# Splitting the attention weights by input tile, with the norm gain folded into the split

## The chip, the cores and the metric

The kernel runs on one core of one Trainium2 chip. The metric is the device time of one execution in microseconds. Engines are named as in the profile: PE is TensorE, with PEld its weight loads; DVE is VectorE, ACT is ScalarE, POOL is GpSimd, and SP issues most DMAs. Each engine runs its instructions in the order in which they were put into its queue.

## The reference

A two-layer decoder trunk over 512 tokens of width 1024. Layer 0 is a gated linear recurrence with a convolutional feed-forward network. Layer 1 is differential attention over shared keys and values, then another such network, then a final norm. What the change touches is layer 1's attention:

```python
def shared_kv(x, kv_norm, kv_w):
    kv = rmsnorm(x, kv_norm) @ kv_w            # keys (8 heads, 2 x 64) and values (8 heads, 128)
...
q = (h @ w_q).reshape(B, T, DA_HEADS, 2, DA_HEAD_DIM) * (DA_HEAD_DIM ** -0.5)
s = jnp.einsum('bqhcd,bkhcd->bhcqk', qb, k) + bias
p = jax.nn.softmax(s, axis=-1)
attn = p[:, :, 0] - lam * p[:, :, 1]
o = jnp.einsum('bhqk,bkhv->bqhv', attn, v)
o = rmsnorm(o, subln_g) * (1.0 - lambda_init)
x = x + o.reshape(B, T, DA_VDIM_TOTAL) @ w_o
```

Here `h` is the stream normed with another gain than that of the keys and values. Both norms are `x * rsqrt(mean(x^2)) * g`, with `g` one factor for each of the 1024 input features. So `g` can be moved from the stream to the rows of the weight that multiplies it.

## The kernel before, in words

**Products in two parts.** Every large product is made from operands split in two: `hi` is the operand rounded to the fast matmul format, `lo` is what the rounding left. Three matmuls, hi x hi, lo x hi and hi x lo (lines 104 to 106), stand for one. The weights come from memory as float32 and are split on the core: ACT casts the high part (`whi`), and DVE subtracts it from the float to get the low part (`wlo`).

**Weights in attention.** One load is a staged tile `wst` of 128 x 1024 (the input features of one of 8 input tiles on the partitions, the columns of all 8 side by side for keys and queries; for values 4 input tiles of 256 columns; for the output weight two output tiles of 4 x 128). `stage` (line 75) issues the DMA on SP. Where a norm gain belongs to the weight, POOL then multiplies the whole tile by it in place (line 86). `Load.high` (line 758) casts all 1024 columns on ACT at line 760, `Load.low` (line 762) subtracts them on DVE at line 763. There are 8 key, 8 query, 8 value and 8 output loads. There are three `wst` buffers and three pairs of `whi` and `wlo`: `high_next` (line 785) begins a split only when fewer than three loads are split or in use.

**The order of the work.** The attention stage is written in one fixed order for PE, DVE, ACT and POOL (line 1039). A block `b` is one head's 128 query tokens; there are 8 x 4 blocks, and block `b % 4 = i` looks at `(i + 1) * 128` keys. In the turn of block `b` the code issues: the scores of block `b + 2` (matmuls, and on DVE the biased minimum at line 968); two units of product work; `weigh(b + 1)`, whose result `at` (line 989, DVE) is the weighted difference of the two softmax parts; `turn(b)`, which transposes `at` on PE (line 996) and copies `aT` to SBUF on ACT (line 998); the exponentials of block `b + 2` on ACT (line 974); three units; `gather(b)`, the product of `aT` and the values on PE (line 1009) with a sum of squares on ACT (line 1012); one unit. After the fourth block of a head, `close` copies the head's output (line 1031) and puts the 13 steps of its norm into a queue `chain` (`ome` at line 1032, `rs` at lines 160 to 166, and so on).

A *unit* is one input tile's part of a key, query, value or output product, three matmuls of 512 columns or six of 256. A key or query product has 8 units, a pair of heads' values 16. `units` (line 941) issues each unit and after it some follow-up work: up to three steps of `chain`, and the casts of keys and queries from the queue `side`. After a key product DVE evacuates it (`kq`, line 833); each of its two halves is cast twice to `kh`, once by ACT into its own partitions (line 854) and once by POOL into the other 64 partitions (line 855); DVE then takes the low parts `kl` (line 861). Queries have two casts on ACT (line 841) and two low parts on DVE (line 844).

The splits stand at fixed places of a block's turn: `low_next` before `turn`, `high_next` after the exponentials, `low_next` after `gather`, and another `high_next` if fewer than two loads are ready. Loads are taken in the order of the list `order`: for each pair of heads two keys and two queries, then the pair's two halves of values; after all pairs the output weights. The first three loads are split ahead of the fixed order, beside the end of the feed-forward stage before it.

Of the kernel before, what the change touches and what calls it, by code (L numbers as in the profile page):

```python
# [19 lines left out]
P = 128  # L20
T = 512
# [15 lines left out]
class Trunk:  # L37
# [34 lines left out]
        self.split(self.x[n], hi, lo, g)  # L72
        return hi, lo

    def stage(self, src, width=1024, gain=None, k0=0, cols=P):

        st = self.wp.tile([P, 1024], F32, tag="wst", name="wst", bufs=3)
        dst = st[:, :width]
        if len(src.shape) == 3:
            dst = dst.rearrange("p (n k) -> p n k", n=src.shape[1])  # L80
        self.nc.sync.dma_start(dst, src)
        if gain is not None:
            n = width // cols
            w = st[:, :width].rearrange("p (k c) -> p k c", k=n)
            g = self.gains[:, gain, k0:k0 + n].unsqueeze(2).broadcast_to([P, n, cols])
            self.nc.gpsimd.tensor_tensor(w, w, g, ALU.mult)
        return st

    def weight_tiles(self):
# [628 lines left out]
    def attention(self, xkv, acc, on_tile):  # L718
        tc, nc, a = self.tc, self.nc, self.a
        v, s = nc.vector, nc.scalar  # L720
        mm = nc.tensor.matmul
        with ExitStack() as ctx:
# [28 lines left out]
            class Load:  # L751
# [1 line left out]
                    me.src, me.gain, me.k0, me.cols = src, gain, k0, cols  # L753

                def stage(me):
                    me.st = self.stage(me.src, 1024, me.gain, me.k0, me.cols)

                def high(me):
                    me.w = self.weight_tiles()
                    s.copy(me.w[0], me.st)  # L760

                def low(me):
                    v.tensor_tensor(me.w[1], me.st, me.w[0].bitcast(F32), ALU.subtract)  # L763

            half = KD // 2

            def out_load(m, k0):
                return Load(a["w_o"][2 * m:2 * m + 2, :, k0 * P:(k0 + half) * P].rearrange("n p k -> p n k"))
# [9 lines left out]
            staged, ready, lows, live, todo = deque(), deque(), deque(), [], deque(order)  # L778

            def stage_next(most=3):  # L780
                while todo and len(staged) < most:
                    staged.append(todo.popleft())
                    staged[-1].stage()

            def high_next():
                if staged and len(live) + len(ready) < 3:
                    ready.append(staged.popleft())
                    ready[-1].high()
                    lows.append(ready[-1].low)

            def low_next():
                while lows:
                    lows.popleft()()

            def split_next():
                high_next()
                low_next()

            def take(load):
                low_next()  # L800
                assert ready and ready[0] is load
                live.append(ready.popleft())
# [28 lines left out]
            def evac(ps, scale=1.0):  # L831
                t = ap.tile([P, T], F32, tag="kq", name="kq")
                v.scalar_tensor_tensor(t, ps, scale, rb, ALU.mult, ALU.mult)
                return t

            def queries(h, ps):

                q = evac(ps, -0.125)
                t = qs[h] = ap.tile([P, 2, T], F32R, tag="qs", name="qs")
                for c, (own, other) in enumerate(parts):  # L840
                    side.append(lambda c=c, own=own: s.copy(t[own, c], q[own]))
                for c, (own, other) in enumerate(parts):
                    side.append(lambda c=c, own=own, other=other:
                                v.tensor_tensor(t[other, c], q[own], t[own, c].bitcast(F32), ALU.subtract))  # L844

            def keys(h, ps):

                k = evac(ps)
                hi = ap.tile([P, 2, T], F32R, tag="kh", name="kh")
                lo = kls[h % 2]  # L850
                ks[h] = hi, lo

                def high(c, own, other):
                    s.copy(hi[own, c], k[own])
                    nc.gpsimd.tensor_copy(hi[other, c], k[own])

                for c, (own, other) in enumerate(parts):
                    side.append(lambda c=c, own=own, other=other: high(c, own, other))
                for c, (own, other) in enumerate(parts):
                    side.append(lambda c=c, own=own:  # L860
                                v.tensor_tensor(lo[own, c], k[own], hi[own, c].bitcast(F32), ALU.subtract))  # L861
# [33 lines left out]
            def add(n, ps):  # L895
                v.tensor_tensor(self.x[n], self.x[n], ps, ALU.add)
# [44 lines left out]
            def units(n, most=1):  # L941
                for _ in range(n):
                    k = next(work, None)
                    if k is None:
                        return
                    if k in (1, 2):
                        stage_next()
                    some(most)


            blocks, heads = {}, {}
# [87 lines left out]
            with tc.manual_schedule(engines=ORDERED):  # L1039
                first = [(self.bank("sc"), take(w[0])) for w in (K[0], Q[0])]  # L1040
                steps, got = self.norm_steps(acc, "n1", "sc")
                self.proj_first(first, xkv, KD - 1, steps)
                live.clear()
                rb, rc = got[1]
                keys(0, first[0][0])
                queries(0, first[1][0])
                some(8)
                units(2)
                split_next()
                units(2)  # L1050
                split_next()
                units(U0 - 4)
                for b in range(-2, 4 * NH):
                    h, i = divmod(b + 2, 4)
                    if h < NH:
                        if i == 0 and h % 2 == 1 and h < NH - 1:
                            bias(h + 1)
                        powers = scores(b + 2)
                    else:
                        powers = lambda: None  # L1060
                    units(U1, 0)
                    if 0 <= b + 1 < 4 * NH:
                        weigh(b + 1)
                    if b < 0:
                        powers()
                        split_next()
                        units(U2 + U3)
                        continue
                    low_next()
                    turn(b)  # L1070
                    powers()
                    high_next()
                    units(U2, 2)
                    gather(b)
# [178 lines left out]
```

## Time and profile before

| | us |
|---|---|
| median of 3 runs | 1269.04 |
| lowest, highest | 1267.32, 1269.81 |
| the profiled execution's own time | 1269.33 |
| its span, first to last instruction | 1267.5 |
| PE busy in the span | 1235.7 |
| DVE busy | 872.0 |
| ACT busy | 569.1 |
| POOL busy | 110.0 |

The profile is that of one execution. The attention stage lies between 640 and 893 us of the span. In the profile's rows a group is written as line, engine, operation, output tile <- input tiles, shapes, count, then busy us and mean ns of one, then the idle time ahead of it and what ended it. A row of the waits reads: who waited, `<-` for whom, us in total, times, longest. A row of the time line reads: start, duration, engine, line, operation, tiles, shapes, count, and in brackets the idle time before it. A row of stretches reads: start and end, length, and for each engine its busy time and instruction count, then the granted TensorE clock (1.00 is full), DMA share and GB/s.

### The profile page before, as it was taken

How to read it: one execution, taken by the hardware profiler on the slowest of the kernel's cores; microseconds unless marked ns; L12 is line 12 of the kernel's file. 1: busy time of each engine (PE TensorE's matmuls, PEld its weight loads, DVE VectorE, ACT ScalarE, POOL GpSimd, SP SyncE). 2: the span in 40 equal slices, each digit the busy share in tenths (PEclk: the TensorE clock that was granted, in tenths of full speed). 3: DMA queues.
4: the chain of work that ended last, by engine and by line, in shares of the span. 5: the costliest groups of instructions: out<-in, count | busy, mean ns of one | idle time of the engine just before them, and what ended most of it. 6: DMA issues, size and time to landing. Idle time of an engine off the chain costs nothing.

```text
span 1267.5 us, 18031 instructions
## 1 busy us (share of the span) xinstructions
PE 1235.7 (97%) x6994; PEld 1043.4 (82%) x6994; DVE 872.0 (69%) x1627; ACT 569.1 (45%) x986; POOL 110.0 (9%) x93
## 2 busy tenths in 40 slices
PE   8999999999999999999999889999999999999997
PEld 7888898788888888888888778798788888888886
DVE  7978879587777777523367988876687777773223
ACT  5454555444444444322245446564454444442221
POOL 3000000020000000000243332201100000000001
PEclk9999999999999999999999899999999999999998
DMA  6223222142333333333322212222233333333322
GB/s 211 84 82 123 85 84 68 38 130 87 97 99 100 100 97 90 100 92 92 96 100 67 72 55 58 77 74 83 84 100 100 89 96 98 100 92 92 96 87 67
DMA packets 37965, 115.36 MB, mean 91 GB/s; under 512 B 4040, under 2 KB 9464, under 8 KB 37880
## 3 DMA queue, kind: packets, MB, share of 16 engines
q1 hardware_dynamic: 36984, 113.30, 29.3%
q8 instruction: 55, 0.90, 0.3%
q10 hardware_dynamic: 896, 0.92, 0.2%
q14 instruction: 30, 0.25, 0.1%
HBM read 112.09 MB, written 3.68 MB: 91 GB/s over the span
## 4 chain that ended last, share of the span: by engine, by line
PE 57%; issue 30%; DVE 9%; ACT 2%; DMA 0%; SPq 0%; POOL 0%; POOLq 0%; ACTq 0%; DVEq 0%
PE mm L106 16%; PE mm L104 16%; PE mm L105 16%; DVE wlo L763 1%; PE po L1009 1%; DVE wlo L60 1%; DVE kl L861 1%; DVE sc L968 1%; PE tp L996 1%; ACT whi L760 1%; PE sc L104 1%; PE sc L105 1%; PE sc L106 1%; DVE sd L459 1%; DVE qs L844 1%
## 5 line engine op out<-in xcount | busy, mean ns | idle before, releaser
L104 PE MATMUL mm<-xh,whi 128*128 128x512 f32 x1008 | 398.7, 396 | 0.1
L105 PE MATMUL mm<-xl,whi 128*128 128x512 f32 x1008 | 394.9, 392 | 2.5 <-DVE xl L63 2.4
L106 PE MATMUL mm<-xh,wlo 128*128 128x512 f32 x1008 | 395.0, 392 | 2.3 <-DVE wlo L60 2.3
L60 DVE TENSOR_TENSOR wlo<-wst,whi 128x1024 fp32r<-128x1024 f32 (+2 forms) x182 | 216.0, 1191 | 152.5 <-ACT whi L59 150.2
L59 ACT CAST whi<-wst 128x1024 fp32r<-128x1024 f32 (+2 forms) x182 | 182.2, 1006 | 239.9 <-PE mm L105 188.1
L106 PEld LDWEIGHTS mm<-xh,wlo 128*128 128x128 f32 x1008 | 189.9, 188 | 43.5 <-DVE wlo L60 3.4
L105 PEld LDWEIGHTS mm<-xl,whi 128*128 128x128 f32 x1008 | 190.3, 189 | 41.6 <-DVE xl L63 4.5
L104 PEld LDWEIGHTS mm<-xh,whi 128*128 128x128 f32 x1008 | 190.3, 189 | 38.1 <-ACT whi L59 0.4
L104 PE MATMUL mm<-hh,whi 128*128 128x512 f32 (+1 forms) x374 | 141.0, 377 | 0.0
L105 PE MATMUL mm<-hl,whi 128*128 128x512 f32 (+1 forms) x374 | 140.8, 377 | 0.0
L106 PE MATMUL mm<-hh,wlo 128*128 128x512 f32 (+1 forms) x374 | 140.8, 376 | 0.0
L669 DVE TENSOR_TENSOR u<-mm,rbc_f 128x512 f32<-128x512 f32 x88 | 60.2, 688 | 73.4 <-PE mm L106 73.4
L149 POOL TENSOR_TENSOR acc<-acc,sq 128x512 f32<-128x512 f32 x18 | 26.7, 1485 | 651.4 <-ACT sq L148 651.2
L105 PEld LDWEIGHTS mm<-hl,whi 128*128 128x128 f32 x374 | 70.4, 188 | 13.0
L104 PEld LDWEIGHTS mm<-hh,whi 128*128 128x128 f32 x374 | 70.4, 188 | 12.9
L106 PEld LDWEIGHTS mm<-hh,wlo 128*128 128x128 f32 x374 | 70.4, 188 | 12.8
L671 ACT ACTIVATE c<-u,pack 128x512 f32<-128x512 f32 x88 | 71.7, 819 | 7.8 <-DVE u L669 4.0
L104 PE MATMUL mm<-whi,xh 128*128 128x256 f32 x256 | 74.0, 290 | 0.0
L59 ACT CAST hh<-c 128x512 fp32r<-128x512 f32 x44 | 27.3, 621 | 102.9 <-DVE c L680 102.9
L105 PE MATMUL mm<-wlo,xh 128*128 128x256 f32 x256 | 72.6, 284 | 0.6 <-DVE wlo L763 0.6
L106 PE MATMUL mm<-whi,xl 128*128 128x256 f32 x256 | 72.5, 284 | 0.0
L673 DVE SCALAR_TENSOR_TENSOR c<-u,pack,c 128x512 f32<-128x512 f32 x88 | 66.1, 751 | 2.8
(259 smaller groups left out, 1714.1 us busy)
## 6 DMA issues: line engine op xcount, KB each, us to landing
wst<-in_w_up_dram SPq DMA_DIRECT2D x88, 512.0 KB, 3.6
wst<-in_w_down_dram SPq DMA_DIRECT2D x32, 512.0 KB, 3.5
wst<-in_w_fqg_dram SPq DMA_DIRECT2D x22, 512.0 KB, 3.8
wst<-in_w_kq_dram SPq DMA_DIRECT2D x16, 512.0 KB, 3.6
wst<-in_w_down_dram SPq DMA_DIRECT2D x16, 384.0 KB, 3.1
wst<-in_w_i_dram SPq DMA_DIRECT2D x8, 512.0 KB, 3.8
wst<-in_w_ao_dram SPq DMA_DIRECT2D x8, 512.0 KB, 3.7
wst<-in_w_v_dram SPq DMA_DIRECT2D x8, 512.0 KB, 3.8
```

The lines of the kernel that those rows point to most:

```text
L59: i = nc.scalar.copy(hi, x)
L60: j = nc.vector.tensor_tensor(lo, x, hi.bitcast(F32), ALU.subtract)
L104: mm(out, s[0], m[0], start=start, stop=False)
L105: mm(out, s[0], m[1], start=False, stop=False)
L106: mm(out, s[1], m[0], start=False, stop=stop)
L149: add = lambda engine=nc.vector: engine.tensor_tensor(acc, acc, sq, ALU.add)
L459: v.copy_predicated(dst, m, src)
L669: v.tensor_tensor(u[:, 2:], ps, rb, ALU.mult)
L671: s.activation(c, u[:, 2:], AF.Identity, bias=self.cb[:, layer, n:n + 1], scale=w(2))
L673: v.scalar_tensor_tensor(c, u[:, 0:T], w(0), c, ALU.mult, ALU.add)
L760: s.copy(me.w[0], me.st)
L763: v.tensor_tensor(me.w[1], me.st, me.w[0].bitcast(F32), ALU.subtract)
```

## The change

POOL no longer multiplies the weights by the gain, and no longer casts keys. A load is split in pieces, one for each input tile (128 columns for keys and queries, 256 for values; output weights, which have no gain, in two pieces of 512). ACT makes a high piece as `Identity(gain * wst)`, DVE a low piece as `gain * wst - whi`. `begin` takes the buffers of a load; `pieces` issues a given number of steps, a step being the next high piece and, one high piece later, a low piece. Each unit is followed by one step, and each block's turn has two more after `gather`; what is left when a product needs its load is issued at once by `take`. The casts of keys into the other 64 partitions go to ACT.

```diff
-    def stage(self, src, width=1024, gain=None, k0=0, cols=P):
+    def stage(self, src, width=1024):
...
-        if gain is not None:
-            n = width // cols
-            w = st[:, :width].rearrange("p (k c) -> p k c", k=n)
-            g = self.gains[:, gain, k0:k0 + n].unsqueeze(2).broadcast_to([P, n, cols])
-            self.nc.gpsimd.tensor_tensor(w, w, g, ALU.mult)
...
+                def begin(me):
+                    me.w = self.weight_tiles()
+                    me.highs = deque(range(1024 // me.cols))
+                    me.lows = deque(me.highs)
+
+                def place(me, k):
+                    g = 1.0 if me.gain is None else self.gain(me.gain, me.k0 + k)
+                    return (slice(k * me.cols, (k + 1) * me.cols), g)
 
                 def high(me):
-                    me.w = self.weight_tiles()
-                    s.copy(me.w[0], me.st)
+                    c, g = me.place(me.highs.popleft())
+                    s.activation(me.w[0][:, c], me.st[:, c], AF.Identity, scale=g)
 
                 def low(me):
-                    v.tensor_tensor(me.w[1], me.st, me.w[0].bitcast(F32), ALU.subtract)
+                    c, g = me.place(me.lows.popleft())
+                    v.scalar_tensor_tensor(me.w[1][:, c], me.st[:, c], g, me.w[0][:, c].bitcast(F32),
+                                           ALU.mult, ALU.subtract)
...
-                return Load(a["w_o"][...].rearrange("n p k -> p n k"))
+                return Load(a["w_o"][...].rearrange("n p k -> p n k"), cols=T)
...
-            def high_next():
+            def begin_next():
                 if staged and len(live) + len(ready) < 3:
                     ready.append(staged.popleft())
-                    ready[-1].high()
-                    lows.append(ready[-1].low)
-            def low_next():
-                while lows:
-                    lows.popleft()()
+                    ready[-1].begin()
+            def pieces(load, most):
+                for _ in range(most):
+                    if load.highs:
+                        load.high()
+                        if len(load.lows) - len(load.highs) < 2:
+                            continue
+                    if load.lows:
+                        load.low()
+            def pieces_next(most=1):
+                begin_next()
+                load = next((n for n in ready if n.lows), None)
+                if load is not None:
+                    pieces(load, most)
             def split_next():
-                high_next()
-                low_next()
+                begin_next()
+                for load in ready:
+                    pieces(load, 1024)
             def take(load):
-                low_next()
                 assert ready and ready[0] is load
+                pieces(load, 1024)
                 live.append(ready.popleft())
...
                 def high(c, own, other):
                     s.copy(hi[own, c], k[own])
-                    nc.gpsimd.tensor_copy(hi[other, c], k[own])
+                    s.copy(hi[other, c], k[own])
...
                     some(most)
+                    pieces_next()
...
-                    low_next()
                     turn(b)
                     powers()
-                    high_next()
                     units(U2, 2)
                     gather(b)
-                    low_next()
                     if b % 4 == 1 and b > 1:
                         back()
-                    if len(ready) < 2:
-                        high_next()
+                    pieces_next(2)
```

More of the change, by code (lines that the diff above doesn't have):

```diff
@@ L755, in stage @@
                 def stage(me):
-                    me.st = self.stage(me.src, 1024, me.gain, me.k0, me.cols)
+                    me.st = self.stage(me.src)
+                def begin(me):
[5 more added lines that the diff above has]
+                    return (slice(k * me.cols, (k + 1) * me.cols), g)
                 def high(me):
-                    me.w = self.weight_tiles()
-                    s.copy(me.w[0], me.st)
+                    c, g = me.place(me.highs.popleft())
+                    s.activation(me.w[0][:, c], me.st[:, c], AF.Identity, scale=g)
                 def low(me):
-                    v.tensor_tensor(me.w[1], me.st, me.w[0].bitcast(F32), ALU.subtract)
+                    c, g = me.place(me.lows.popleft())
+                    v.scalar_tensor_tensor(me.w[1][:, c], me.st[:, c], g, me.w[0][:, c].bitcast(F32),
+                                           ALU.mult, ALU.subtract)
             half = KD // 2
             def out_load(m, k0):
-                return Load(a["w_o"][2 * m:2 * m + 2, :, k0 * P:(k0 + half) * P].rearrange("n p k -> p n k"))
+                return Load(a["w_o"][2 * m:2 * m + 2, :, k0 * P:(k0 + half) * P].rearrange("n p k -> p n k"), cols=T)
             K = [[Load(a["w_kq"][2 * h], 2)] for h in range(NH)]
@@ L777, in attention @@
             order += O[0] + O[1]
-            staged, ready, lows, live, todo = deque(), deque(), deque(), [], deque(order)
+            staged, ready, live, todo = deque(), deque(), [], deque(order)
             def stage_next(most=3):
```

## The prediction

> **What bounds the kernel now.** I read the page first, then the waits of TensorE in the attention stage, then the time line where the waits lie, and last the groups of DVE and ACT in one stretch between them.
>
> ```profile
> PE 1235.7 (97%) x6994; PEld 1043.4 (82%) x6994; DVE 872.0 (69%) x1627; ACT 569.1 (45%) x986; POOL 110.0 (9%) x93
> ```
>
> TensorE is the bound. The edited code runs in the attention stage alone (640 to 893 us), so the change can only give back what TensorE loses there. Its waits in that window:
>
> ```profile
> PE tp L996 <- DVE at L989: 9.5, 5, 3.0
> PE po L1009 <- ACT aT L998: 3.8, 3, 1.5
> PE mm L105 <- DVE wlo L763: 0.6, 1, 0.6
> ```
>
> Together 13.9 us. After some of these waits the clock is low for a while, as the first two stretches below show (columns: PE, PEld, DVE, ACT, POOL busy; granted clock; DMA). The third holds the key and query products of one pair of heads.
>
> ```profile
> 672.10:675.30 3.20, 3.12 (x9) 2.54 (x10) 1.98 (x10) 1.40 (x5) 0.00 (x0) 0.53 0.00 0
> 704.90:714.30 9.40, 8.56 (x31) 6.96 (x32) 8.83 (x27) 6.40 (x15) 0.00 (x0) 0.64 0.26 75
> 737.20:774.40 37.20, 32.93 (x182) 27.70 (x182) 32.40 (x78) 20.75 (x56) 13.22 (x8) 1.00 0.25 69
> ```
>
> The clock costs at most (1 - 0.53) x 3.2 = 1.5 us and (1 - 0.64) x 9.4 = 3.4 us, 4.9 in all. Part of it falls into waiting, so I take 3. The ceiling of a gain is 13.9 + 4.9 = 18.8 us, my central value for it 16.9.
>
> Why does `at` come late? The longest wait of TensorE (2.96 us, ended at 705.03) with GpSimd and DVE before it:
>
> ```profile
> 705.03 0.44 PE L996 MATMUL tp<-pack,at 128*128 128x128 f32 x2 [2.96 <-DVE at L989]
> ...
> 693.23 1.89 POOL L86 TENSOR_TENSOR wst<-wst,gains 128x1024 f32<-128x1024 f32 x1 [4.55 <-DVE wlo L763]
> 695.18 2.51 POOL L855 CAST kh<-kq 64x512 fp32r<-64x512 f32 x2
> 697.77 4.07 POOL L86 TENSOR_TENSOR wst<-wst,gains 128x1024 f32<-128x1024 f32 x2
> ...
> 691.90 1.22 DVE L763 TENSOR_TENSOR wlo<-wst,whi 128x1024 fp32r<-128x1024 f32 x1
> 693.48 2.73 DVE L763 TENSOR_TENSOR wlo<-wst,whi 128x1024 fp32r<-128x1024 f32 x1 [0.35 <-ACT whi L760]
> 696.12 2.11 DVE L861 TENSOR_TENSOR kl<-kq,kh 64x512 fp32r<-64x512 f32 x2
> 698.27 1.75 DVE L1032 TENSOR_SCALAR ome<-oms 128x4 f32<-128x4 f32 x1
> 700.05 1.82 DVE L160 TENSOR_SCALAR rs<-ome 128x4 int32<-128x4 int32 x1
> 704.49 0.48 DVE L989 SCALAR_TENSOR_TENSOR at<-p,r 128x256 f32<-128x256 f32 x1
> ```
>
> Against the same operations where GpSimd is idle:
>
> ```profile
> 727.70 0.17 DVE L1032 TENSOR_SCALAR ome<-oms 128x4 f32<-128x4 f32 x1
> 727.90 0.17 DVE L160 TENSOR_SCALAR rs<-ome 128x4 int32<-128x4 int32 x1
> ...
> 768.18 1.40 DVE L861 TENSOR_TENSOR kl<-kq,kh 64x512 fp32r<-64x512 f32 x2
> ```
>
> A 128x4 operation takes 1.75 us instead of 0.17 while GpSimd multiplies, and a whole low part takes 2.73 us instead of 1.22. In the ten us shown DVE loses 1.51 + (2.11 - 1.40 = 0.71) + 1.58 + 1.65 = 5.5 us this way, more than the 2.96 us that TensorE waited. So DVE is the engine that comes late, in lumps.
>
> The other kind of wait is on ACT, which runs in order: at 707.73 a whole high part stands ahead of `aT`, and `qs` before it had waited for the late DVE.
>
> ```profile
> 706.08 1.26 ACT L841 CAST qs<-kq 64x512 fp32r<-64x512 f32 x2 [2.14 <-DVE kq L833]
> 707.73 1.03 ACT L760 CAST whi<-wst 128x1024 fp32r<-128x1024 f32 x1
> 708.66 0.37 ACT L998 COPY aT<-tp 128x256 f32<-128x256 f32 x1
> ```
>
> **The change, costed in one stretch.** I take the third stretch, two key and two query products. The waits of TensorE in it:
>
> ```profile
> PE tp L996 <- DVE at L989: 2.7, 1, 2.7
> PE po L1009 <- ACT aT L998: 1.5, 1, 1.5
> ```
>
> So its own need is 37.2 - 4.2 = 33.0 us. What do DVE and ACT need there afterwards? Their groups in it, and below them the rows of other places that give prices:
>
> ```profile
> L763 DVE TENSOR_TENSOR wlo<-wst,whi 128x1024 fp32r<-128x1024 f32 x5 | 8.3, 1652 | 2.9 <-ACT whi L760 2.9
> L861 DVE TENSOR_TENSOR kl<-kq,kh 64x512 fp32r<-64x512 f32 x4 | 3.4, 862 | 0.1
> L160 DVE TENSOR_SCALAR rs<-ome 128x4 int32<-128x4 int32 x1 | 1.9, 1850 | 0.0
> L1032 DVE TENSOR_SCALAR ome<-oms 128x4 f32<-128x4 f32 x1 | 1.7, 1748 | 0.0
> L989 DVE SCALAR_TENSOR_TENSOR at<-p,r 128x128 f32<-128x128 f32 x2 | 0.7, 353 | 0.1
> L989 DVE SCALAR_TENSOR_TENSOR at<-p,r 128x256 f32<-128x256 f32 x1 | 0.5, 485 | 0.0
> ...
> L760 ACT CAST whi<-wst 128x1024 fp32r<-128x1024 f32 x6 | 6.3, 1046 | 0.0
> L854 ACT CAST kh<-kq 64x512 fp32r<-64x512 f32 x4 | 2.5, 621 | 1.6 <-DVE kq L833 1.5
> ...
> L578 ACT ACTIVATE xg<-x,gains 128x512 f32<-128x512 f32 x7 | 5.0, 709 | 0.0
> L578 ACT ACTIVATE xg<-x,gains 128x256 f32<-128x256 f32 x2 | 1.0, 494 | 0.0
> ...
> 661.05 0.36 ACT L974 ACTIVATE p<-sc,stat 128x128 f32<-128x128 f32 x1
> 661.31 0.19 ACT L974 ACTIVATION_READ_ACCUMULATOR p<-sc,stat 128x1 f32 x1
> ...
> 659.80 0.68 DVE L833 SCALAR_TENSOR_TENSOR kq<-mm,rbc_n 128x512 f32<-128x512 f32 x1
> 660.40 0.29 DVE L968 CUSTOM_DVE_ANT_0 sc<-sc,nb 128x128 f32<-128x128 f32 x1
> ```
>
> *Price of a piece on DVE.* `at` is the same operation with the same kinds of operands as a new low piece: 0.353 us at 128 columns, 0.485 at 256. The next operation starts 0.08 us before the last one ends where nothing holds it (659.80 + 0.68 against 660.40). So a piece holds DVE for 0.27 or 0.40 us, and for 0.35 or 0.49 at most.
>
> *Price of a piece on ACT.* `xg` multiplies by a gain per partition from SBUF: 0.709 at 512 columns and 0.494 at 256. One more halving takes off 0.107, so 0.39 at 128 (an estimate from these two rows). The overlap is 0.10 us (661.05 + 0.36 against 661.31). So 0.29 or 0.39 us, and 0.39 or 0.49 at most.
>
> *DVE.* Five loads are split in the stretch, three of keys or queries (8 pieces each) and two of values (4 each), by the order list and the three weight buffers. Removed: 8.3 for five whole low parts; 3.4 - 4 x 0.70 = 0.6 of stretching in `kl`; 1.75 + 1.85 - 2 x 0.17 = 3.3 in `ome` and `rs`. Added: 24 x 0.27 + 8 x 0.40 = 9.7. So 32.4 - 12.2 + 9.7 = 29.9 us, under the 33.0 of TensorE, and in small parts, not lumps. At full price it is 24 x 0.35 + 8 x 0.49 = 12.3 and 32.5 us.
>
> *ACT.* Removed: 6.3 for whole high parts. Added: 24 x 0.29 + 8 x 0.39 = 10.1, and four key copies taken over from GpSimd, 4 x 0.62 = 2.5. So 20.75 - 6.3 + 12.6 = 27.1 us of 33.0; at full price 13.3 for the pieces and 30.3 us. ACT has room, but in order: it must also sit through waits for TensorE, and all casts of a key stand ahead of the next `aT`.
>
> The Trainium skill speaks against the small parts: its page "VectorE: DVE Perf Modes", section on the TRN2 errata, says that an operation from SBUF pays a fixed latency each time and advises tiles of 512 elements or more. By that rule the sums at full price would hold, and the result is the second case below; this trace has the 0.10 and 0.08 us of overlap beside it.
>
> *At no cost.* The multiplication on GpSimd leaves the path from the weight DMA to ACT, which gains only at the start, since GpSimd mostly waited for the DMA. The first three loads are split under the end of the feed-forward stage, while ACT and DVE sit idle between products; without that cover it is 3 x 8 x 0.29 = 7 us. Output weights go in two pieces of 512, 0.62 each against 1.05 for the whole, with no wait of TensorE in that part now. A staging buffer is held for about eight units longer. What queues behind a held load on SP is the next load and a bias tile, needed a product and four blocks later; the cover is the three loads staged ahead. A first piece into a reused buffer waits on ACT for the product that still reads it; behind it stand `aT` and `powers`, which follow TensorE anyway. DVE's low part comes one piece behind ACT's high, so it rarely waits.
>
> **The sum.** The waits of 13.9 us go, with 3 us of slow clock. What is late next is ACT: `aT` already ended 3.8 us of waits, and I let that much stand as new waits, since ACT goes from 20.75 to 27 us in the stretch. Change: -13.9 - 3 + 3.8 = -13.1 us. The profiled execution took 1269.33 us (span 1267.5), the median is 1269.04, 0.3 lower. So about 1256 us.
>
> **The rivals.**
>
> *ACT and DVE nearly full.* The pieces stand between waits and never overlap, so they cost full price: DVE 32.5 and ACT 30.3 of 33.0 us. For it: ACT must wait in line (the row below). Against it: the overlaps above. About half of the waits then stay: -13.9 / 2 - 1.5 = -8.5, so 1261 us (1258 to 1266).
>
> ```profile
> ACT aT L998 <- PE tp L996: 38.1, 25, 2.5
> ```
>
> *Nothing gained.* The change does not do what it says: DVE's long operations are not due to GpSimd, and the 0.6 + 3.3 = 3.9 us of stretching in `kl`, `ome` and `rs` stay. Then DVE needs 29.9 + 3.9 = 33.8 us against 33.0, and the waits stay where they are: 1266.5 to 1271.5. Against it speak the pairs of rows above; for it only that the trace names GpSimd nowhere as the one who releases DVE.
>
> *Slower: ACT comes late at each gather.* At full price ACT gets 13.3 - 6.3 + 2.5 = 9.5 us more in a stretch, which holds about 32 units of six to a block, 5.3 blocks: 1.8 us a block, ahead of that block's `aT`. Today ACT waits 38.1 / 25 = 1.5 us for `tp` before `aT`, a reserve that takes nearly all of it. Where ACT meets a late evacuation in line (`qs` waited 2.14 us above) the reserve is gone. In three such stretches, 16 gathers, TensorE would wait up to 16 x 1.8 = 29 us against 16.9 gained: +12, 1281 us. It breaks even at 16.9 / 16 = 1.1 us a gather, that is at a reserve of 0.7 us; under that it is slower (1272 to 1281).
>
> **How the numbers follow.** First case (1250 to 1260) 0.62, nearly full 0.18, nothing gained 0.08, slower 0.12. A measurement of this kernel tells about 0.2%, 2.5 us, from no change. Faster: 0.62 + 0.18 = 0.80; same 0.08; slower 0.12. The range goes from the whole ceiling (1269 - 18.8 = 1250) over the second case into the third, to 1268. That leaves out the slower case, half of the third and little else.
>
> **What would show it.** In the profile of the changed kernel: no GpSimd multiplications in attention, `ome` and `rs` at 0.17 us and `kl` at 0.70 throughout; low pieces of about 0.35 us and high pieces of about 0.39; the waits of `tp` for `at` near zero (under 2 us in total); the clock at 1.00 from 672 to 715; the waits of `po` for `aT` between 0 and 5 us. Wrong if `po` waits over 8 us for `aT`, if a new wait of a product for `whi` or `wlo` stands high, or if `at` still comes late with GpSimd silent.

## The result, and the profile after

| | before | after |
|---|---|---|
| median, us | 1268.18 (4 runs) | 1276.56 (4 runs) |
| lowest, highest | 1264.74, 1269.81 | 1276.0, 1278.27 |
| the profiled execution | 1269.33 (span 1267.5) | 1276.37 (span 1274.4) |

The ratio after to before is 1.0075 (95% interval 1.0061 to 1.0089): the kernel became slower by some 9.5 us, where a gain of 13 was forecast.

The page's first part, of the kernel after:

```profile
PE 1236.4 (97%) x6994; PEld 1044.7 (82%) x6994; DVE 858.0 (67%) x1771; ACT 606.4 (48%) x1146; POOL 45.4 (4%) x53
```

TensorE has the same work (1235.7 before), so the time went into its waits or its clock. DVE is down by 14 us, ACT up by 37, POOL down by 65: the work moved as the change says. TensorE's waits in the attention stage of the kernel after, for the row of three waits that the prediction showed of before:

```profile
PE po L1028 <- ACT aT L1017: 13.6, 6, 3.0
PE tp L1015 <- DVE yl L1048: 3.3, 3, 1.1
PE mm L99 <- ACT vt L906: 2.6, 1, 2.6
```

No wait for `at` is left, and none for a piece. In their place `po` waits for `aT` at six gathers, and there are two kinds of wait that the prediction doesn't name: `tp` for `yl`, and a product for `vt`. Together 19.5 us, against 13.9. What follows such waits in the clock shows in stretches of 20 us (columns as in the prediction), of the kernel after, all those with a clock under 1.00:

```profile
650.00:670.00 20.00, 17.39 (x102) 15.15 (x100) 13.71 (x37) 15.09 (x37) 0.00 (x0) 0.96 0.26 79
670.00:690.00 20.00, 20.00 (x123) 17.87 (x122) 13.39 (x47) 12.89 (x43) 0.00 (x0) 0.96 0.09 27
...
710.00:730.00 20.00, 16.60 (x107) 15.29 (x108) 14.96 (x54) 13.98 (x41) 0.00 (x0) 0.91 0.24 71
...
770.00:790.00 20.00, 19.78 (x140) 18.91 (x141) 15.34 (x55) 12.47 (x41) 0.00 (x0) 0.91 0.18 53
...
810.00:830.00 20.00, 14.36 (x70) 11.35 (x69) 15.14 (x44) 13.97 (x38) 0.00 (x0) 0.91 0.24 80
```

And of the kernel before, likewise all those with a clock under 1.00:

```profile
670.00:690.00 20.00, 18.14 (x109) 16.06 (x108) 13.64 (x35) 11.13 (x31) 4.28 (x4) 0.91 0.09 27
690.00:710.00 20.00, 16.33 (x77) 12.95 (x76) 18.49 (x43) 9.89 (x25) 8.41 (x5) 0.91 0.26 79
710.00:730.00 20.00, 20.00 (x131) 18.55 (x131) 17.48 (x39) 11.74 (x32) 6.27 (x5) 0.92 0.31 93
```

The low clock costs 20 x (0.04 + 0.04 + 0.09 + 0.09 + 0.09) = 7.0 us at most after, since part of it falls into waiting, and 20 x (0.09 + 0.09 + 0.08) = 5.2 before (4.9 by the prediction's two stretches). Waits and clock together: 19.5 + 7.0 = 26.5 against 13.9 + 5.2 = 19.1, that is +7.4 us; the spans of the two executions differ by 1274.4 - 1267.5 = 6.9. So the waits of TensorE in attention and the clock behind them account for the loss.

The stretch of the kernel after that stands nearest to 737.2 to 774.4 of before, and its groups of DVE and ACT:

```profile
737.20:775.40 38.20, 32.56 (x163) 26.73 (x163) 29.14 (x101) 26.93 (x81) 0.53 (x1) 0.96 0.24 69
```

```profile
L768 DVE SCALAR_TENSOR_TENSOR wlo<-wst,gains,whi 128x128 fp32r<-128x128 f32 x24 | 7.6, 348 | 2.4 <-ACT whi L764 2.4
L768 DVE SCALAR_TENSOR_TENSOR wlo<-wst,gains,whi 128x256 fp32r<-128x256 f32 x8 | 3.5, 480 | 2.6 <-ACT whi L764 2.6
L879 DVE TENSOR_TENSOR kl<-kq,kh 64x512 fp32r<-64x512 f32 x4 | 2.7, 685 | 1.2 <-ACT kh L872 1.2
L764 ACT ACTIVATE whi<-wst,gains 128x128 fp32r<-128x128 f32 x25 | 8.4, 395 | 3.2 <-issue 3.2
L764 ACT ACTIVATE whi<-wst,gains 128x256 fp32r<-128x256 f32 x8 | 3.6, 500 | 0.0
...
L872 ACT CAST kh<-kq 64x512 fp32r<-64x512 f32 x4 | 2.5, 616 | 1.8 <-DVE kq L851 1.8
L859 ACT CAST qs<-kq 64x512 fp32r<-64x512 f32 x2 | 1.2, 618 | 2.3 <-DVE kq L851 2.3
```

The prediction's prices were right (0.348 and 0.480 us on DVE, 0.395 and 0.500 on ACT), and its counts up to one piece. Its sums look right too: DVE 29.1 us (29.9 forecast), ACT 26.9 (27.1). For ACT that is in part luck. Its sum took out six whole high parts and put in the pieces of five loads, and the two stretches don't hold the same work. There are 12 exponentials before and 10 after, two for a block, as these rows of before and then of after count them:

```profile
L974 ACT ACTIVATION_READ_ACCUMULATOR p<-sc,stat 128x1 f32 x12 | 2.4, 201 | 0.0
L993 ACT ACTIVATION_READ_ACCUMULATOR p<-sc,stat 128x1 f32 x10 | 2.0, 200 | 0.0
```

The whole kernel is the fairer test. ACT's busy time rose by 606.4 - 569.1 = 37.3 us; the price with overlap gives 128 x 0.29 + 32 x 0.39 + 16 x 0.62 - 24 x 1.05 = 34.3, the full price 50.3. So the price with overlap held, within a tenth.

Yet TensorE waits 5.6 of the 38.2 us (three times, shown below). The number that misled stands in the idle column: ACT, which must work in order, sits 2.3 + 1.8 = 4.1 us in front of evacuations that are not there yet. With them it is taken for 26.9 + 4.1 = 31.0 of TensorE's 32.6 us. (The 3.2 us of idle time in the row of `whi` lie at the stretch's end, behind its last late gather: the first piece into a reused buffer starts at 775.14, when the last matmul that reads this buffer has just ended.) Standing in line was not new: over the whole stage ACT waited 9.2 + 8.3 us for `kq` before and 7.7 + 7.5 after. New is the work that stands between this wait and `aT`.

How it loses the gather shows in ACT's time line, and below it TensorE's, both of the kernel after:

```profile
763.09 0.68 ACT L1047 ACTIVATE yh<-tp,subg 128x512 fp32r<-128x512 f32 x1
763.66 0.50 ACT L764 ACTIVATE whi<-wst,gains 128x256 fp32r<-128x256 f32 x1
765.97 0.62 ACT L872 CAST kh<-kq 64x512 fp32r<-64x512 f32 x1 [1.81 <-DVE kq L851]
766.60 0.62 ACT L873 CAST kh<-kq 64x512 fp32r<-64x512 f32 x1
767.23 0.61 ACT L872 CAST kh<-kq 64x512 fp32r<-64x512 f32 x1
767.86 0.62 ACT L873 CAST kh<-kq 64x512 fp32r<-64x512 f32 x1
768.50 1.30 ACT L764 ACTIVATE whi<-wst,gains 128x256 fp32r<-128x256 f32 x3
769.71 0.46 ACT L1017 COPY aT<-tp 128x384 f32<-128x384 f32 x1
```

```profile
759.81 0.71 PE L1028 MATMUL po<-vt,aT 128*128 128x128 f32 x4 [1.51 <-ACT aT L1017]
764.61 0.55 PE L1015 MATMUL tp<-pack,at 128*128 128x128 f32 x3 [1.11 <-DVE yl L1048]
770.22 0.99 PE L1028 MATMUL po<-vt,aT 128*128 128x128 f32 x5 [3.01 <-ACT aT L1017]
```

From 764.2 to 766.0 ACT holds still for the keys' evacuation. Then come four casts (two of them from GpSimd) and three pieces, 3.7 us, and only then `aT`: TensorE has waited 3.01 us for it. All six late gathers are of this kind. They come in three pairs: TensorE waits 1.5 us where ACT had stood before `qs`, and 3.0 us where it had stood before `kh`. The wait at 764.61 has the same root: `yh` reads the one `tp` bank, DVE's `yl` follows it and frees it, and `yh` came late on ACT.

### The profile page after: what moved, and what is told of

Read it like the earlier page. It is cut to its first block, busy times and chain, and to the rows that moved or that the text cites. A ratio compares the mean times of both kernels' runs of the same rounds, so it can differ in the third digit from the quotient of the medians.

```text
span 1274.4 us, 18244 instructions
## 1 busy us (share of the span) xinstructions
PE 1236.4 (97%) x6994; PEld 1044.7 (82%) x6994; DVE 858.0 (67%) x1771; ACT 606.4 (48%) x1146; POOL 45.4 (4%) x53
## 4 chain that ended last, share of the span: by engine, by line
PE 57%; issue 30%; DVE 7%; ACT 4%; DMA 0%; POOL 0%; SPq 0%; POOLq 0%; ACTq 0%; DVEq 0%
PE mm L99 16%; PE mm L101 16%; PE mm L100 16%; PE po L1028 1%; ACT whi L764 1%; DVE wlo L768 1%; DVE wlo L60 1%; ACT kh L873 1%; ACT p L993 1%; PE sc L99 1%; PE sc L100 1%; PE sc L985 1%; DVE sd L454 1%; PE sc L101 1%; PE sc L984 1%
## 5 line engine op out<-in xcount | busy, mean ns | idle before, releaser
L768 DVE SCALAR_TENSOR_TENSOR wlo<-wst,gains,whi 128x128 fp32r<-128x128 f32 (+1 forms) x160 | 53.8, 375 | 23.9 <-ACT whi L764 23.5
```

The costliest lines, as they stand in the source:

```text
L768: v.scalar_tensor_tensor(me.w[1][:, c], me.st[:, c], g, me.w[0][:, c].bitcast(F32), ALU.mult, ALU.subtract)
```

## The experiments

Each kernel was timed beside the kernel before, and its ratio to that is given with the 95% interval. Differences in us are differences of ratios times 1267.5. Waits are TensorE's in the attention stage, less the 2 us for `xl` at the start of the next stage, which all kernels have.

My theory after the result: ACT's line is too full ahead of `aT`. Rivals: the collisions with GpSimd were never what cost time (*Nothing gained*); the pieces cost too much wherever they stand; the places of the pieces cost the time.

### E1: the second key casts back on GpSimd

In the kernel after:

```diff
-                    s.copy(hi[other, c], k[own])
+                    nc.gpsimd.tensor_copy(hi[other, c], k[own])
```

> The changed kernel, but the second cast of each key half is back on GpSimd. Theory A (ACT is late because of what stands in its line ahead of aT; the two added casts of 0.62 us are one part of it): the 3.0 us wait of po for aT in each pair falls by about 1.2 us, the 1.5 us wait stays, so 1276.6 - 3 x 1.2 - some slow clock = about 1272 us. Theory B (ACT simply has too much work in a key and query stretch, wherever it stands): ACT gets 2.5 us back in each of three stretches, waits fall by the same, about 1269. Theory C (GpSimd's casts collide with DVE as the multiplications did): kl goes from 0.69 to about 1.1 us, at is late again, 1275 or more.

Measured: 1262.5 us, 0.996 [0.9945, 0.9974], faster than each of the three theories had it. TensorE's waits:

```profile
PE po L1028 <- ACT aT L1017: 6.1, 6, 1.8
PE tp L1015 <- DVE yl L1048: 3.3, 3, 1.1
```

The 16 casts, 16 x 0.62 = 10 us of ACT, cost 14.6 us of the kernel, and more than half of the waits for `aT` go with them. The rest of the change is a small gain.

### E2: no pieces ahead of `aT`

In the kernel after, units before the turn and behind the gather issue no step; three steps stand directly behind the exponentials.

```diff
-                    pieces_next()
+                    if step:
+                        pieces_next()
...
-                    units(U1, 0)
+                    units(U1, 0, b < 0)
...
                     powers()
+                    pieces_next(3)
...
-                    pieces_next(2)
...
-                    units(U3, 2)
+                    units(U3, 2, False)
```

> The changed kernel with its pieces placed otherwise: none in the two units ahead of turn and none between gather and the next turn, three directly behind the exponentials, and one with each of the three units behind that. The amount of work on ACT is the same. Theory A (place): ahead of the late aT of each pair stood six pieces (1.8 us) and three value pieces (1.2 us); the 1.5 us waits go, the 3.0 us waits fall to about 1.8, the waits of tp for yl (1.1) fall or go: 1276.6 - 3 x 3.8 = about 1265 us. Theory B (amount): no gain, 1275 to 1278, the waits only move.

Measured: 1276.57 us, 1.0066 [1.0045, 1.0086]. No gain, but other waits:

```profile
PE tp L1016 <- DVE yl L1049: 6.1, 3, 2.2
PE po L1029 <- ACT aT L1018: 3.6, 4, 1.3
PE mm L100 <- DVE wlo L768: 3.5, 3, 1.2
PE mm L99 <- ACT vt L906: 2.6, 1, 2.6
PE mm L101 <- DVE wlo L768: 2.4, 3, 0.8
```

The waits for `aT` fall from 13.6 to 3.6, so the pieces ahead of it do delay it. But pieces now came late for their own product (the waits for `wlo`), and `yl` later still. The time is what theory B had. The run leaves open what the places cost.

### E3, E4 and E7: the whole splits, without GpSimd

Three edits of the kernel before. E3: GpSimd doesn't multiply; the gain is left out. E4: GpSimd doesn't cast keys, ACT does. E7: both, so that GpSimd does nothing there.

```diff
-                    me.st = self.stage(me.src, 1024, me.gain, me.k0, me.cols)
+                    me.st = self.stage(me.src, 1024)
...
-                    nc.gpsimd.tensor_copy(hi[other, c], k[own])
+                    s.copy(hi[other, c], k[own])
```

E3, the first pair of lines:

> The kernel before, whole splits, with the multiplication of the weights by the gain left out altogether (so the output is not scaled by it); GpSimd still casts keys. It shows what the multiplications on GpSimd cost before. If they are the cause of the late at (the prediction's reading): ome and rs at 0.17, wlo at 1.22 us, most of the 9.5 us of waits for at go, and 3 us of slow clock: 1257 to 1260 us. If not: 1266 to 1270.

E4, the second pair:

> The kernel before, whole splits and the multiplications on GpSimd, with the second cast of each key half on ACT as in the change: that part of the change alone. Theory A: two more casts of 0.62 us ahead of aT after each key product, but DVE's kl is free of GpSimd's casts: between -3 and +4 us against before, 1265 to 1272. If the added casts alone explain the loss of the change: 1274 or more.

E7, both:

> The kernel before with whole splits, without the multiplication by the gain (left out, so the output is not scaled by it), and with the second casts of keys on ACT: GpSimd has no part in the attention's blocks, and ACT about 23 us of work in a stretch. If casts on ACT cost only where pieces stand there as well (theory B): 1248 to 1252, as without the multiplications and with GpSimd's casts (1249.9). If the casts cost 1.2 us a key product by themselves: 1255 to 1260.

Measured: E3 1249.86 us, 0.9859 [0.9842, 0.9876]; E4 1263.59, 0.9969 [0.9959, 0.998]; E7 1252.86, 0.9894 [0.9879, 0.9908]. TensorE's waits in E7:

```profile
PE po L1009 <- ACT aT L998: 1.8, 3, 0.6
PE mm L105 <- DVE wlo L763: 0.3, 1, 0.3
PE mm L104 <- ACT vt L888: 0.2, 1, 0.2
```

So the collision was real, and worth about what was forecast: without its multiplications the kernel gains 17.9 us (E3, where TensorE has no wait but `xl`; the sum had 16.9). Nor are the casts free on ACT: E7, which moves them there, gains 13.4, that is 4.5 less. Where GpSimd still multiplies (E4) the same move gains 3.9 us, so the added casts alone don't explain the loss. *Nothing gained* is out. The low key parts show the collision over the whole stage, in before and then in after (min, median and max in ns), and so does `ome`, here in after (1.75 us in before):

```profile
L861 DVE TENSOR_TENSOR kl<-kq,kh x16: 676/992/2376, 652.8 to 819.3; 64x512 fp32r<-64x512 f32 x16
```

```profile
L879 DVE TENSOR_TENSOR kl<-kq,kh x16: 676/687/690, 652.9 to 825.9; 64x512 fp32r<-64x512 f32 x16
```

```profile
750.76 0.16 DVE L1051 TENSOR_SCALAR ome<-oms 128x4 f32<-128x4 f32 x1
```

E3 and E4 tell GpSimd's two kinds of work apart: beside its casts alone `kl` takes 991 ns at most (E3), beside its multiplications alone up to 2435 (E4).

The Trainium skill has a rule for this, in its page "GPSIMD Engine Reference", section "Specifications": GpSimd shares its SBUF interfaces with VectorE, and they contend where DVE's instruction has two SBUF inputs or runs in a 2-port performance mode. `kl` has two, and the trace agrees: up to 2376 ns beside GpSimd, 690 at most without it. `ome` has one SBUF input and is stretched all the same; in which mode it runs, no run here shows.

### E5 and E10: keys and queries cast after the next unit

In the kernel after (E5) and in E1 (E10), a unit's follow-up work (the casts of `side` with their low parts on DVE, and the steps of `chain`) is issued ahead of the next unit, not directly behind its own, and so behind the piece between the two. They are the same instructions, in another order.

```diff
                 for _ in range(n):
+                    some(most)
                     k = next(work, None)
...
-                    some(most)
                     pieces_next()
```

> The changed kernel with the follow-up work of a unit (casts of keys and queries) issued ahead of the next unit instead of directly behind its own, so that ACT does not stand waiting for the evacuation of a product that has just ended (2.3 us for a query and 1.8 us for a key in one stretch of the changed kernel). The amount of work on ACT is the same. Theory L (the idle time of ACT in line is what makes it late): up to 4 us of ACT come free in each of three stretches, waits fall by 2 to 4 us each, 1264 to 1270 us. Theory B (the amount of ACT's work alone): no gain, 1274 to 1278.

> The changed kernel with both cures: the second casts of keys back on GpSimd (alone 1262.5) and the follow-up work issued ahead of the next unit (alone 1267.0). If ACT's work and its waits in line add up to its lateness: the 10.0 us of waits left with the casts on GpSimd fall to 4 to 7, 1256 to 1260 us. If the waits that are left have another cause (the single tp bank, freed by yl): no gain, 1261 to 1263.

Measured: E5 1267.02 us, 0.9999 [0.999, 1.0009]; E10 1264.15, 0.9975 [0.9965, 0.9984]. ACT's waits in the kernel after, then in E5, and TensorE's in E5:

```profile
ACT kh L872 <- DVE kq L851: 7.7, 5, 1.8
```

```profile
ACT kh L872 <- DVE kq L851: 0.9, 1, 0.9
```

```profile
PE tp L1015 <- DVE yl L1048: 7.5, 3, 2.5
PE po L1028 <- ACT aT L1017: 5.4, 3, 1.8
```

With not one instruction less, 9.6 us came back: 6.8 us of standing in line before `kh` went, and with it 8.2 us of waits for `aT`. Other waits of ACT moved too: before `qs` from 7.5 to 8.1, before the exponentials from 2.2 to 9.3, and those of first pieces (in the profile's word "issue") from 12.4 to 4.4. So the run shows that these 9.6 us hang on the order, at the same amount of work; it doesn't single out the wait before `kh`. That the wait for `yl` grew from 3.3 to 7.5 in the same run shows the next one in the line. With the casts on GpSimd (E10) the new order gains nothing: `aT` 6.1 to 1.6, `yl` 3.3 to 7.5, and the time is 1.9 us longer than E1 (the intervals overlap). It lies above both ranges expected.

### E6: one of the two extra casts on GpSimd

```diff
-                    s.copy(hi[other, c], k[own])
+                    (s.copy if c else nc.gpsimd.tensor_copy)(hi[other, c], k[own])
```

> The changed kernel with one of the two added casts of a key product on ACT and the other on GpSimd: half the dose between 1276.6 (both on ACT) and 1262.5 (both on GpSimd). If each us on ACT past a point is paid by TensorE (theory B): halfway, about 1269. If there is a threshold (the slow clock that follows waits of 2 us and more): nearer to 1263, 1263 to 1266.

Measured: 1268.72 us, 1.0021 [1.001, 1.0033], with 9.9 us of waits for `aT`. That is +2.7 us, halfway between E1 (-5.1) and the kernel after (+9.5): half the casts bring half of the loss, which speaks against a reserve in ACT's line that has to be used up first. Nor does the clock show a clean threshold: in before it fell to 0.53 behind a wait of 1.9 us (672.2), and was 1.00 from 750 to 770 us, where TensorE waited 2.7 us (758.8).

### E11: the high part whole, at the first step

The kernel after, but the high part is one cast without gain; the low parts stay in pieces (times one).

```diff
-                    c, g = me.place(me.highs.popleft())
-                    s.activation(me.w[0][:, c], me.st[:, c], AF.Identity, scale=g)
+                    if me.highs.popleft() == 0:
+                        s.copy(me.w[0], me.st)
```

> The changed kernel with the low parts in pieces on DVE and all casts of keys on ACT, but the high part whole, in one cast at the load's first step and without the gain (left out, so the output is not scaled by it). ACT gets about 4.4 us less in a stretch; DVE does the same work as in the change. If the pieces on ACT are what the change loses by: near the kernel without GpSimd and with whole splits (1252.9), 1252 to 1257. If the pieces on DVE or their number is the loss: 1265 or more.

Measured: 1272.08 us, 1.0041 [1.0028, 1.0054]; waits for `aT` 6.3, for `yl` 5.9 us, in an execution of 1276.58 us, the longest of this kernel. ACT has less work, but the whole cast into a reused buffer now stands before the product that still reads it, in E11 and, for comparison, in the kernel after:

```profile
ACT whi L764 <- PE mm L100: 20.0, 7, 4.4
```

```profile
ACT whi L764 <- PE mm L100: 4.7, 3, 1.8
```

So E11 doesn't tell the price of ACT's pieces. It suggests that a wait in ACT's line does the same harm as work.

### E13 to E16: pieces in a row, at the old places

From E7: E13 makes ACT's high parts of keys, queries and values in pieces with the gain, E14 DVE's low parts without it, E15 both with their gain. Here the pieces of a load stand together where the whole split stood before. E15 has all the work of the change, on the same engines (only the output weights stay whole). E16 is E15 with the second key casts on GpSimd.

```diff
-                    s.copy(me.w[0], me.st)
+                    if me.gain is None:
+                        s.copy(me.w[0], me.st)
+                        return
+                    for k in range(1024 // me.cols):
+                        c = slice(k * me.cols, (k + 1) * me.cols)
+                        s.activation(me.w[0][:, c], me.st[:, c], AF.Identity, scale=self.gain(me.gain, me.k0 + k))
```

> Whole splits at their old places, nothing on GpSimd, casts of keys on ACT (1252.9 us), but the high part of key, query and value loads in pieces times the gain, all pieces of a load in a row at the old place of the high part. Low parts whole, without the gain (left out in the low part, so the output is off). ACT's work is that of the change. Theory M (the amount of work on ACT makes the waits): 1265 us or more. Theory P (their places do: strewn one by one, and directly behind a product whose buffer they take): 1253 to 1259.

> The same kernel with the low part in pieces instead, in a row at the old place of the low part, and the high part whole; the gain left out in both, so the output is not scaled by it. DVE's work is that of the change, ACT's that of the kernel without pieces. Theory M: 1252 to 1257, DVE has room. Theory P: the same. If pieces on DVE are the loss (the whole high part with low pieces took 1272): 1265 or more.

> Both in pieces with the gain, at the old places, casts of keys on ACT: the work of the changed kernel on every engine, nothing left out, only the pieces of a load in a row at the old places instead of one with each unit. Theory M: 1270 to 1278, as the change. Theory P: 1254 to 1262.

> The same, with the second casts of keys on GpSimd. Theory M: near 1262, as with pieces one by one and these casts on GpSimd (1262.5). Theory P: 1252 to 1258.

Measured: E13 1264.23 us, 0.9974 [0.9962, 0.9986]; E14 1259.31, 0.9937 [0.9919, 0.9954]; E15 1264.0, 0.9967 [0.9957, 0.9977]; E16 1261.29, 0.995 [0.9934, 0.9966]. TensorE's waits in E15:

```profile
PE po L1021 <- ACT aT L1010: 6.4, 5, 1.8
PE mm L104 <- ACT vt L900: 2.6, 1, 2.6
```

Together 9.0 us, against 2.3 in E7 and 19.5 in the kernel after, and no wait for `yl`. E13 and E14 alone lose 10.1 and 5.4 us on E7, E15 9.3: the two don't add up, and the runs don't say why. Neither theory has the times right: E13 lies just under M's and above P's, E14 above both, E15 between them, E16 near M's. So the pieces cost time in a row at the old places too, and their strewn places are only a part of the loss. Four kernels with all the pieces make a table, as difference from before:

| us | casts on GpSimd | casts on ACT |
|---|---|---|
| pieces in a row, old places | -6.3 (E16) | -4.2 (E15) |
| one step with each unit | -5.1 (E1) | +9.5 (after) |

The casts on ACT cost 2.1 us where the pieces stand together, and 14.6 where they are spread. The spreading costs 1.2 us with the casts on GpSimd and 13.7 with them on ACT. (At the two small differences the intervals overlap.) Neither the casts nor the spreading makes the loss alone; it takes the two together.

### E8, E9 and E12: the gain in the activations

From the kernel before, the gain of keys and values is put into the split of their shared input `x`, which is there anyway: eight high parts on ACT at 0.72 us with a gain in place of 0.62 without, and eight low parts on DVE. Query weights alone are multiplied on GpSimd, by the ratio of the two gains (so no gain may be zero). All of the reference is computed. E9 is E8 with a filler of 144 in place of 152 floats, so that tiles behind it lie 32 bytes lower.

```diff
-            K = [[Load(a["w_kq"][2 * h], 2)] for h in range(NH)]
+            K = [[Load(a["w_kq"][2 * h])] for h in range(NH)]
...
-            V = [[Load(a["w_v"][p, hf], 2, 4 * hf, 256) for hf in range(2)] for p in range(NH // 2)]
+            V = [[Load(a["w_v"][p, hf]) for hf in range(2)] for p in range(NH // 2)]
...
-        xs, acc, nxt = nxt[0], nxt[1], stage("plain")
+        xs, acc, nxt = nxt[0], nxt[1], stage(2)
```

> The kernel before, but the gain of the keys and values is multiplied into the stream where it is split (one scale operand in 16 operations that are there anyway), so that key and value weights need none; GpSimd multiplies only the 8 query loads, by the ratio of the two gains. Whole splits, casts as before. 16 of 24 multiplications on GpSimd go. If these cost 16.7 us together (1266.6 against 1249.9 without them) and evenly: 1255.5; 1251 to 1260.

> The kernel with the gain of keys and values in the stream (1258.3 us), with one padding constant smaller by 8, so that the new tile of 8 floats (32 bytes a partition) shifts no other tile. In that kernel a 128x512 matmul came every 233.3 ns in the feed-forward stages, where all other kernels have 226.7, over some 240 us, which is 7 us. If the shift of addresses is the cause: 226.7 ns again, 1250 to 1253 us. If not: 1258.

Measured: E8 1258.32 us, 0.994 [0.9925, 0.9955]; E9 1250.8, 0.9869 [0.9852, 0.9885]. E9 beats both kernels, by 16.6 us and 26 us. It has one wait besides `xl`:

```profile
PE mm L105 <- DVE wlo L766: 0.6, 1, 0.6
```

E12 is the kernel after with E9's gain in `x` and filler: query weights alone are in pieces on ACT and DVE, spread over the units, key and value loads are split whole at a unit's step, and the casts are E10's:

> The gain of keys and values in the stream, so that key and value loads are split whole; query loads alone in pieces times the ratio of the two gains on ACT and DVE; second casts of keys on GpSimd, which does nothing else; follow-up work issued ahead of the next unit; the same padding as above. No multiplication on GpSimd, and ACT has only 8 of 24 loads in pieces: about 2 us less in a stretch than with all in pieces. If both causes are read rightly this is near the kernel without the multiplications (1249.9): 1249 to 1253 us.

Measured: 1254.88 us, 0.99 [0.9885, 0.9915]; waits for `yl` 2.7 us. It is 3.9 us slower than E9. Pieces for a third of the loads that have a gain bring nothing over GpSimd's multiplication of these. How much of the 3.9 us comes from the order of the casts (1.9 us in E10) or from the whole high parts at a unit's step (as in E11), this run doesn't say.

## Why the prediction was wrong

**What held.** That GpSimd's work stretches DVE's, and that this makes `at` late: E3 and E7 give 17.9 and 13.4 us for it, and after the change `at` is never waited for. The prices of the pieces and DVE's sum held within 3%; ACT's sum came out within 1%, in part by luck, as shown above.

**The step that failed** is "ACT has room, but in order", and from it "I let that much stand as new waits": the term +3.8 of the sum. It measured 19.5 us, and 7.0 us of low clock where the sum took most of the low clock as gone. The room was taken as 33.0 - 27.1 = 5.9 us of a stretch. ACT spends 4.1 of it standing before `qs` and `kh`, in line, and what is left is not at the gathers. The prediction had that wait in its hands (2.14 us for `qs`) and used it in its slower rival, not in the sum. The 3.8 us about cover what the casts alone cost (4.5, E3 against E7); for what the pieces add in ACT's line the sum had nothing. Its own sign of being wrong, over 8 us of `po` for `aT`, showed: 13.6.

**How the 13 us were lost,** by ratios: nothing on GpSimd -13.4 (E7); all the pieces in a row +9.3, to -4.2 (E15); the pieces spread over the units +13.7, to +9.5 (after). The second term is the piecework: 16 x 8 + 8 x 4 = 160 pieces on ACT and as many on DVE, in E15 as in the change. The Trainium skill's rule that the prediction weighed ("VectorE: DVE Perf Modes", section on the TRN2 errata: many small operations pay a fixed latency each) points this way. But the pieces came at the price with overlap, not at the full price, and ACT's alone in a row lost 10.1 us (E13). So the time was lost without a dearer piece; by E15's waits, of which 6.4 in 9.0 us are for `aT`, most of it went to what stands ahead of `aT`. The third term is mostly the order of work: E5 takes back 9.6 us with the same instructions.

**The rivals.** *Slower: ACT comes late at each gather* had the mechanism, the victim and the size (1272 to 1281; 1276.6 measured). It was off in the number: 6 gathers waited and not 16, each 2.3 us on average and not 1.8, and the rest came from `yl`, `vt` and the clock. Its chance of 0.12 was too low: the reserve before `aT` was taken from a mean over 25 waits, but it was the gathers behind an in-line wait that counted. *Nearly full* had DVE and ACT at full price; they measured the lower one. *Nothing gained* is refuted by E3 and E7.

**At no cost.** "no wait of TensorE in that part now" held for the output weights. "DVE's low part comes one piece behind ACT's high, so it rarely waits" did not: it cost DVE 2.4 + 2.6 us of idle time in the stretch, and TensorE no wait. The start is no later either: the first `kl` stands at 652.9 us, against 652.8 before. That a first piece waits for the product that still reads its buffer was put at nothing; in the change none of the late gathers stands behind such a wait, in E11, with the whole high part there, it was 20.0 us of ACT.

**What stays open:** how the 13.7 us of spreading divide between pieces ahead of `aT`, the wait in line ahead of both, and the late `yh` on the one `tp` bank, since each edit that removed one of them made another longer (E2, E5, E10); and why E13 and E14 don't add up to E15.

## What to carry to other kernels

Busy time short of a full stretch is no room on an engine that works in order: add its waits in line to its work, and look at what stands between such a wait and the one instruction that the bounding engine waits for. Two moves of work to the same engine can each be nearly free and dear together, so try them apart and together. Before splitting an operation to move a scale factor, look for a place where the factor can be put into an instruction that exists anyway: that gave 16.6 us here (E9), with eight instructions of ACT longer by 0.10 us and no other work moved there.

## What the runs showed of the hardware

**A shift of 32 bytes changes the pace of some matmuls.** E8's attention stage is as short as E9's (232.7 and 232.2 us from the last matmul on `hh` to the last on `yh`, 252.4 in before), yet the kernel is 9 us slower, by the ratios 0.994 and 0.9869. Of the 7.8 us between the two profiled spans some 6.2 lie in products that the edit doesn't touch, the second of each feed-forward network (528 and 594 matmuls on `hh` and `hl`). The same 60 us of the first one, ahead of attention, in E8 and then in E9, both with the clock at 1.00:

```profile
560.00:620.00 60.00, 60.00 (x258) 48.18 (x258) 17.89 (x20) 16.73 (x20) 5.18 (x4) 1.00 0.32 97
```

```profile
560.00:620.00 60.00, 60.00 (x267) 49.67 (x266) 18.87 (x20) 16.77 (x20) 5.23 (x4) 1.00 0.32 97
```

A matmul comes every 60 / 258 = 233 ns in E8 and every 60 / 267 = 225 in E9. The kernel before has E9's pace there (226 ns). The filler's size is the only edit between the two. Which tile's address matters was not tried.
